# Kurtosis of 1,024 rows on one Trainium2 core: the queue by which the last results leave

## The chip, the core and the metric

The kernel runs on one core of a Trainium2 chip. Its time is device microseconds of that core for one execution, and a kernel's time is the median of several executions. The profile is of one execution. Its engines are TensorE (PE for matmuls, PEld for weight loads), VectorE (DVE), ScalarE (ACT), GpSimd (POOL) and SyncE (SP), which here only issues transfers and waits. A "q" behind an engine's name (SPq, ACTq) is the part of the engine that waits and issues, whose time isn't counted as busy.

## What is computed

The input is x, 1,024 rows of 8,192 float32 values, 33.5 MB. The output has one float32 for each row, 4 KB in all.

```
mean = np.mean(x, axis=-1, keepdims=True)
std = np.std(x, axis=-1, keepdims=True)
z = (x - mean) / (std + 1e-8)
return (np.mean(z ** 4, axis=-1) - 3).astype(np.float32)
```

So each row needs its mean, the sum of squares of the centred values, and the sum of their fourth powers. The whole input must be read once, and the output is four small stores.

## The kernel before, in words

The rows are cut into 18 groups (`GROUPS`). A group of k parts holds 128/k rows, each row cut into k pieces on k partitions, so that a group fills all 128 partitions with 8192/k columns. The first three groups have k = 8, 8 and 4 (less data, so that work starts early), the other fifteen k = 2, that is 64 rows and 4,096 columns each. A group is loaded into one of five buffers (`xt0` to `xt4`) by one to four transfers, all issued by SP (line 126). SP waits until a buffer is free, and that order is written out by hand in `load_next`.

For every group three things are done:

- The mean. In early groups DVE adds the two halves of the columns (line 149); in later ones PE transposes and sums 128-column blocks into PSUM (line 132) and DVE reduces pairs (line 138). A matmul with a small constant matrix gives minus the mean for each partition (lines 159 to 168), and ACT copies it to SBUF (line 170).
- The square. ACT computes (x - mean)^2 in place and keeps the sum (line 176).
- The fourth power. DVE squares and sums most of the columns (line 188), ACT the rest (line 183).

Results are put together for batches of groups (`BATCHES`): groups 0 and 1, group 2, groups 3 to 12, and groups 13 to 17. `factor` sums the squares of a row's pieces by matmul (lines 200 to 204) and takes minus the inverse square on DVE (lines 206 and 208). `scaled` multiplies the fourth-power sums by it (lines 215 and 216). `result` sums the pieces of a row by matmul with a selection matrix (line 226), subtracts 3 on DVE into the tile `kr` (line 228), and SP stores `kr` to `out` (line 230). For the last batch `kr` is 5 partitions of 64 values, 1.2 KB.

The batches before the last one are finished in steps between the groups. The last batch stands by itself at the end: ACT squares group 17 in two halves, DVE takes the fourth powers, ACT scales its share into `wa` (line 282), DVE its share into `w4` (line 284), and `result(b, [wa, w4])` accumulates both by two matmuls.

Line 313 of the profile is the end of the program, where the scope of the kernel is left. There SP waits for the eight semaphores on which transfers report, five wait instructions in all, and for DVE and ACT. In both builds the last of the five wait instructions holds the semaphore of the last store and the DVE count that comes with `kr`; the others hold semaphores of earlier transfers. Then all engines meet: each signals GpSimd, GpSimd releases them, the semaphores are cleared, and they meet again.

The statement that sets what the change touches is, in `result`:

```
nc.vector.tensor_scalar_add(kr, pk, -3.0)
dst = out[ROWS[b[0]]:ROWS[b[-1] + 1]].rearrange("(g r) -> g r", r=r)
nc.sync.dma_start(out=dst, in_=kr)
```

Of the kernel before, what the change touches and what calls it, by code (L numbers as in the profile page):

```python
# [43 lines left out]
def kernel(  # L44
# [5 lines left out]
    nc = tc.nc  # L50
# [4 lines left out]
    L = NG - 1  # L55
# [32 lines left out]
    for k in dict.fromkeys(k for k in KS if k > 2):  # L88
# [4 lines left out]
        out=ident, in_=ident, pattern=[[-1, P]], base=0,  # L93
# [125 lines left out]
    def result(b, terms):  # L219
        n = len(b)  # L220
        k = KS[b[0]]
        r = P // k
        sel = blk[k].rearrange("p (r k) -> p r k", k=k)[:, :, 0]
        pk = psfin.tile([n, r], f32, name="pk")
        for j, t in enumerate(terms):
            nc.tensor.matmul(pk, lhsT=t, rhs=sel, start=j == 0, stop=j == len(terms) - 1)  # L226
        kr = fin.tile([n, r], f32, name="kr")
        nc.vector.tensor_scalar_add(kr, pk, -3.0)  # L228
        dst = out[ROWS[b[0]]:ROWS[b[-1] + 1]].rearrange("(g r) -> g r", r=r)
        nc.sync.dma_start(out=dst, in_=kr)  # L230

    def finish(b):
        fac = factor(b)
        yield
        w4 = scaled(b, fac, len(b))
        yield
        result(b, [w4])
# [18 lines left out]
    for i in range(L):  # L256
# [12 lines left out]
    b = BATCHES[-1]  # L269
# [15 lines left out]
        out=w4[:, n - 1:], in0=qd[:, n:], scalar=qd[:, n - 1:n], in1=fac[:, n - 1:],  # L285
        op0=AO.add, op1=AO.mult)
    result(b, [wa, w4])


# [28 lines left out]
```

## Time and profile before

| what | value |
|---|---|
| median of 5 runs | 97.81 us (97.47 to 98.31) |
| the profiled execution's own time | 97.66 us |
| its span, first to last instruction | 95.9 us (95.943) |
| around the span | 1.72 us |
| ACT busy | 79.7 us, 83% |
| DVE busy | 76.2 us, 79% |
| PE busy | 57.4 us, 60% |
| HBM read | 33.55 MB, 350 GB/s over the span |
| last input packet | at 84.2 us |
| end of the last compute instruction (`kr`, line 228) | 93.9 us |

The views used are these. The page's slices cut the span in 40 equal parts with a digit for each engine's busy share. The chain of work that ended last follows the end of the program back through what released each step. The timeline lists instructions by start, with their length in us. The waits name who waited for whom: total us, times, longest. The list of a line gives the lengths of its instructions as minimum, median and maximum in ns. Starts and ends with three decimals are from the same trace's records, among them the landings: the moments at which a transfer's completion reaches its semaphore.

### The profile page before, as it was taken

The numbers are of one execution on the slowest core, as the hardware profiler recorded it, in microseconds if no ns is written. First come the engines' busy times: TensorE is split into PE (matmuls) and PEld (weight loads), VectorE is DVE, ScalarE is ACT, GpSimd is POOL, SyncE is SP. The second block draws the span as 40 slices with busy tenths as digits, with TensorE's granted clock in tenths as the row PEclk, the third lists the DMA queues.
The fourth block names the chain that finished last, engine by engine and source line by source line (L and its number), as shares of the span: only waits on it lengthen the run. The fifth ranks groups of instructions, "written<-read, shape, count | busy, mean of one in ns | idle before, by whom it ended". The sixth has DMA issues, their size and how long they took to land.

```text
span 95.9 us, 1268 instructions
## 1 busy us (share of the span) xinstructions
PE 57.4 (60%) x440; PEld 52.1 (54%) x440; DVE 76.2 (79%) x86; ACT 79.7 (83%) x89; POOL 4.6 (5%) x19
## 2 busy tenths in 40 slices
PE   0040202020299797979797979797978797961230
PEld 0040202020299696969696969696867686850210
DVE  2239449899992485989898989797989796999980
ACT  6055621999999499999999999999999898899960
POOL 6930000000000000000000000000000000000000
PEclk9999999999999999999999999999999999999655
DMA  2999999999999999999999999999999999400000
GB/s 68 377 398 454 437 430 437 430 424 395 407 409 393 439 421 431 423 422 412 432 412 435 417 409 421 401 419 410 418 413 418 407 418 406 171 3 0 0 0 4
DMA packets 5226, 33.63 MB, mean 351 GB/s; under 512 B 612, under 2 KB 612, under 8 KB 3812
## 3 DMA queue, kind: packets, MB, share of 16 engines
q1 hardware_dynamic: 5220, 33.56, 84.9%
q8 instruction: 3, 0.05, 0.2%
q14 instruction: 3, 0.02, 0.1%
HBM read 33.55 MB, written 0.00 MB: 350 GB/s over the span
## 4 chain that ended last, share of the span: by engine, by line
DMA 37%; ACT 25%; DVE 18%; PE 12%; issue 6%; SPq 0%; DVEq 0%
DMA xt<-in_x_dram 37%; ACT xt L176 21%; DVE xt L188 10%; PE tps L132 9%; DVE junk L149 6%; ACT xt L183 2%; PE mps L159 1%; PE mps L168 1%; DVE red L138 1%; ACT nmu L170 1%; PE pk L226 1%; ACT wa L282 0%; DVE qd L188 0%; DVE kr L228 0%; DVE fac L208 0%
## 5 line engine op out<-in xcount | busy, mean ns | idle before, releaser
L176 ACT ACTIVATE xt<-xt,nmu 128x4096 f32<-128x4096 f32 (+2 forms) x19 | 60.4, 3178 | 0.6
L188 DVE CUSTOM_DVE_ANT_0 xt<-xt 128x3456 f32<-128x3456 f32 (+7 forms) x19 | 58.9, 3102 | 1.7 <-ACT nmu L170 1.0
L132 PE MATMUL tps<-ident,xt 128*128 128x128 f32 x380 | 47.6, 284 | 0.5 <-DMA xt<-in_x_dram 0.3
L132 PEld LDWEIGHTS tps<-ident,xt 128*128 128x128 f32 x380 | 44.3, 148 | 2.1 <-DMA xt<-in_x_dram 1.8
L159 PE MATMUL mps<-part,blk 128*128 128x1 f32 x12 | 3.4, 350 | 23.1 <-DVE part L149 23.1
L159 PEld LDWEIGHTS mps<-part,blk 128*128 128x128 f32 x12 | 3.0, 311 | 23.4 <-ACT xt L176 9.2
L149 DVE CUSTOM_DVE_ANT_0 junk<-xt 128x2048 bf16<-128x2048 f32 (+3 forms) x7 | 10.0, 1427 | 6.3 <-DMA xt<-in_x_dram 6.3
L183 ACT ACTIVATE xt<-xt 128x640 f32<-128x640 f32 (+5 forms) x15 | 12.9, 858 | 0.5
L170 ACT COPY nmu<-mps 128x1 f32<-128x1 f32 x18 | 2.7, 150 | 11.2 <-PE mps L159 9.0
L138 DVE TENSOR_REDUCE red<-tps 128x128 f32<-128x256 f32 x12 | 5.1, 425 | 8.0 <-PE tps L132 7.9
L168 PEld LDWEIGHTS mps<-negcol,red 128*128 128x128 f32 x22 | 3.3, 188 | 8.9 <-ACT xt L176 5.7
L168 PE MATMUL mps<-negcol,red 128*128 128x1 f32 x22 | 3.9, 247 | 6.6 <-ACT xt L176 3.0
L176 ACT ACTIVATION_READ_ACCUMULATOR xt<-xt,nmu 128x1 f32 x19 | 3.5, 185 | 0.0
L183 ACT ACTIVATION_READ_ACCUMULATOR xt<-xt 128x1 f32 x15 | 2.8, 186 | 0.0
L70 ACT ACT_TABLE_LOAD x1 | 1.3, 1283 | 0.8 <-PEq L302 0.8
L83 POOL TENSOR_SCALAR_AFFINE_SELECT blk<-blk 128x128 f32<-128x128 f32 x3 | 1.7, 562 | 0.2
L80 POOL TENSOR_SCALAR_AFFINE_SELECT blk<-blk 128x128 f32<-128x128 f32 x3 | 1.7, 554 | 0.2
L201 PE MATMUL p<-s,blk 128*128 128x1 f32 x2 | 0.4, 260 | 2.1 <-ACT xt L176 2.1
L188 DVE DVE_READ_ACCUMULATOR2_ANT qd<- 128x1 f32 x19 | 1.6, 83 | 0.0
L202 PE MATMUL p<-s,blk 128*128 128x1 f32 x2 | 0.6, 363 | 1.6 <-ACT xt L176 1.6
L201 PEld LDWEIGHTS p<-s,blk 128*128 128x128 f32 x2 | 0.3, 188 | 2.2 <-ACT xt L176 2.2
L202 PEld LDWEIGHTS p<-s,blk 128*128 128x128 f32 x2 | 0.5, 313 | 1.7 <-ACT xt L176 1.7
(32 smaller groups left out, 13.0 us busy)
## 6 DMA issues: line engine op xcount, KB each, us to landing
xt<-in_x_dram SPq DMA_DIRECT2D x7, 1152.0 KB, 10.8
xt<-in_x_dram SPq DMA_DIRECT2D x9, 768.0 KB, 11.6
xt<-in_x_dram SPq DMA_DIRECT2D x7, 896.0 KB, 12.6
xt<-in_x_dram SPq DMA_DIRECT2D x3, 2048.0 KB, 11.0
xt<-in_x_dram SPq DMA_DIRECT2D x6, 512.0 KB, 11.3
xt<-in_x_dram SPq DMA_DIRECT2D x1, 1024.0 KB, 6.5
xt<-in_x_dram SPq DMA_DIRECT2D x1, 640.0 KB, 11.8
xt<-in_x_dram SPq DMA_DIRECT2D x1, 384.0 KB, 10.8
```

The costliest lines, as they stand in the source:

```text
L70: nc.scalar.activation(out=zeros[:, :1], in_=zeros[:, :1], func=AF.Square)
L80: nc.gpsimd.affine_select(out=v, in_=v, pattern=[[-k, r], [0, k]], base=0, channel_multiplier=1, compare_op=AO.is_ge, fill=0.0)
L83: nc.gpsimd.affine_select(out=v, in_=v, pattern=[[k, r], [0, k]], base=k - 1, channel_multiplier=-1, compare_op=AO.is_ge, fill=0.0)
L132: nc.tensor.matmul(tps, lhsT=xts[i][:, c:c + P], rhs=ident, start=c == 0, stop=c == w - P, is_transpose=True)
L138: nc.vector.tensor_reduce(out=red.rearrange("p (r k) -> p r k", k=2), in_=tps.rearrange("p (r k) -> p r k", k=2).unsqueeze(2).to_broadcast ...
L149: nc.vector.tensor_tensor_reduce(out=junk[:, :h], in0=t[:, :h], in1=t[:, h:], scale=1.0, scalar=0.0, op0=AO.add, op1=AO.add, accum_out=part)
L159: nc.tensor.matmul(mps, lhsT=blk[k], rhs=added_halves(i, 0), start=True, stop=True)
L168: nc.tensor.matmul(mps, lhsT=pair_sums(tps), rhs=negcol, start=True, stop=True)
L170: nc.scalar.copy(nmu, mps)
L176: nc.scalar.activation(out=t, in_=t, func=AF.Square, bias=nmus[i], accum_out=s2[:, j + extra:j + extra + 1])
L183: nc.scalar.activation(out=t, in_=t, func=AF.Square, accum_out=qa[:, j:j + 1])
L188: nc.vector.tensor_tensor_reduce(out=t, in0=t, in1=t, scale=1.0, scalar=0.0, op0=AO.mult, op1=AO.add, accum_out=qd[:, j + extra:j + extra ...
```

## The change

The store of the last batch is issued by ScalarE instead of SyncE. `b[-1] == L` holds for the batch that contains the last group alone; the three earlier stores stay with SyncE.

```diff
         dst = out[ROWS[b[0]]:ROWS[b[-1] + 1]].rearrange("(g r) -> g r", r=r)
-        nc.sync.dma_start(out=dst, in_=kr)
+        queue = nc.scalar if b[-1] == L else nc.sync
+        queue.dma_start(out=dst, in_=kr)
```

All lines behind it move down by one (282 becomes 283, 313 becomes 314). In the built program, the transfer becomes the last instruction of ACT before the end of the program, behind the scaling into `wa`; the semaphore that it reports on and the count that it waits for are as before. From SP's list the transfer goes, and with it a wait for that semaphore's earlier use. No other engine's order changes.

## The prediction

> **What bounds the kernel now.** I read the page's slices first, to see which stage the change is in; then the chain that ended last and the timeline of the last 4 us, for what stands on the path; then SP's waits, for who is late at the end; then the lengths of issues, for prices. The slices:
>
> ```profile
> DVE  2239449899992485989898989797989796999980
> ACT  6055621999999499999999999999999898899960
> DMA  2999999999999999999999999999999999400000
> GB/s 68 377 398 454 437 430 437 430 424 395 407 409 393 439 421 431 423 422 412 432 412 435 417 409 421 401 419 410 418 413 418 407 418 406 171 3 0 0 0 4
> ```
>
> The first 84 us are the loads with ACT and DVE beside them, the next 10 the arithmetic of the last groups, and in the last slice (2.4 us) ACT and DVE stand at 0, under a tenth. The change touches only that slice. The store that it moves is issued at 93.9 us, and by then the transfers have been idle for nearly ten us. So the loads, the buffers and the arithmetic keep their times, and what matters is the stretch from the last compute instruction to the end. The timeline of it (start us, length us, engine, line):
>
> ```profile
> 92.55 0.29 ACT L282 ACTIVATE wa<-qa,fac 128x1 f32<-128x1 f32 x1
> ...
> 93.29 0.38 PE L226 MATMUL pk<-blk,w 128*5 128x64 f32 x2
> 93.70 0.21 DVE L228 TENSOR_SCALAR kr<-pk 5x64 f32<-5x64 f32 x1 [0.47 <-PE pk L226]
> 93.94 0.29 SPq L230 DMA_DIRECT2D out_dram<-kr  x1
> ```
>
> `kr` ends at 93.910, its signal comes at 93.922, SP begins to issue at 93.938 (16 ns later) and is done at 94.231. ACT has nothing after 92.85. The packets, in a window from 93 to 97 us, whose 40 slices are 0.1 us each:
>
> ```profile
> DMA  0000000000000000000000002000000000000000
> GB/s 0 0 0 0 0 0 0 0 0 0 0 0 0 0 0 0 0 13 0 0 0 0 0 0 82 0 0 0 0 0 0 0 0 0 0 0 0 0 0 0
> ```
>
> The store's packets are the 13 in the slice from 94.7 (first packet 94.705, 0.474 us after the issue's end); the 82 at 95.5 is a fetch of instructions, which nobody waits for. The landings are at 95.047 to 95.103. What SP then waits for, from 75 us on (us in total, times, longest):
>
> ```profile
> SPq L230 <- DVE kr L228: 18.6, 2, 13.5
> SPq L313 <- PEq L313: 0.6, 2, 0.4
> SPq L313 <- DMA out_dram<-kr: 0.2, 1, 0.2
> ```
>
> The third row is the one to see: of its five waits at the end, SP stands only 0.2 us for the store itself. The four waits before it fill 94.277 to 94.886 and end 0.217 us ahead of the last landing (95.103 - 94.886). So the path is: `kr` signal 93.922; start 0.016; issue 0.293; to the first packet 0.474; to the last landing 0.398; SP passes its last wait at 95.119; from there to the span's end 95.943 is 0.824 us in which the engines meet.
>
> **The change part by part.** Each term is a difference to that path.
>
> 1. Start. ACT waits for the same DVE count. The nearest row is ACT's wait ahead of line 282: `fac`'s signal is at 92.242, ACT's wait record starts at 92.263, 21 ns later against SP's 16. Cost +0.005 us. Nothing is queued behind ACT's transfer but its signal at the meeting. This has cover: GpSimd needs all signals, SP's comes at 95.26, and ACT's issue would end near 94.24. Even with an issue of 1.06 us it ends at 95.0, and then the landing, which SP waits for, is later still. Without the cover, ACT's next instructions (17 and 14 ns) would cost under 0.1.
>
> 2. Issue. The page has no issue by ACT. The nearest rows are SP's own:
>
> ```profile
> L230 SPq DMA_DIRECT2D out_dram<-kr x4: 264/308/335, 52.3 to 93.9; - x4
> L126 SPq DMA_DIRECT2D xt<-in_x_dram x36: 327/328/1057, 0.8 to 74.5; - x36
> ```
>
> Lower bound: the shortest, 264 ns, is -0.029 against the 293 replaced. I see no reason why ACT should go under it. Upper bound: the longest, 1,057 ns, +0.764. A first use need not be slow: SP's first four loads took 402, 420, 419 and 432 ns, the first the shortest. I take the row nearest in shape, the store that is replaced: 0.
>
> 3. The queue. The page's DMA table has only q1 (SP's) and two queues of instructions; ACT's has not carried a packet. Nearest row: SP's first transfer, also on an unused queue, starts at 0.799, is issued in 402 ns and has its first packet at 1.844, 0.643 us after the issue's end. The last store needs 0.474. The difference, +0.169, is all that this trace has for an unused queue; it can be due to 128 partitions instead of 5, or to reading HBM instead of SBUF. Bounds: 0 and, if the issue's extra length counts too, +0.278 (1.045 - 0.767 from issue start to packet). I take +0.169, as the one row with an unused queue.
>
> The Trainium skill, "DMA: Bandwidth & Descriptors", section "Issuing engines are not separate DMA queues", says that transfers started by different engines run on the same 16 DMA engines and that a second issuer saves only issue time. Its section "Queues, rings and completion order" gives SP and ACT each a row of rings on those engines. By the first rule alone the store would cost what it does now, a change of 0, with nothing to save since SP has no other issue after 80.4; no run here shows it yet.
>
> 4. What SP loses: its issue, and a wait at 80.40 for the earlier use of the semaphore. SP can then run its four earlier waits as their transfers land, the last of them at 84.635, and stand at the fifth from then on. That takes 94.277 to 94.886 off SP, but this work is beside the store's flight already: gain 0, and at most nothing while the landing is later than 94.886. After the landing SP does the same five steps, 0.824 us.
>
> Other edits: none. ACT has one instruction more, SP two fewer.
>
> **Sum.** +0.005 + 0 + 0.169 + 0 = +0.17 us. Against the profiled execution: 97.66 + 0.17 = 97.83. That execution was 0.15 under the median; the change touches none of what may differ between executions, so I add the same sum to the median: 97.81 + 0.17 = 97.98. Half a per cent is 0.49 us, about what a measurement of this kernel can tell from no change. The forecast is inside it. Its own range comes from the bounds, -0.03 to +0.28, and 0.2 for a median's wander among runs spread from 97.47 to 98.31: 97.6 to 98.3.
>
> **The rivals.**
>
> - ACT's first issue is slow (slower than before). ACT has run only arithmetic for 94 us, and this would be the one transfer of its life in the program. For: no row shows an ACT issue, and SP once needed 1,057 ns where its neighbours took 328, so an issue is not bound to 0.3. Against: that long one fell beside a fetch of instructions (16 KB, from 41.518 on for 1.08 us), and SP's own first one was not long. Nothing covers it: every ns goes into the landing, and thence into the end. Price: 0.764 + 0.005 + 0.169 = +0.94, 98.75; with the queue's upper bound 1.05, 98.86. It decides from an issue of 0.293 + (0.49 - 0.17) = 0.61 us.
> - SP's work at the end is the bound (faster). If in other executions the landing comes before SP has done its four waits, or if the 1.72 us around the span hold work that hangs on SP's last transfer, then a free SP ends sooner. For: SP's four waits include one stall of 0.42 us (94.434 to 94.858), for which none of their semaphores is the cause, since these had been met by 84.64. Against: the third row of the waits has the landing last by 0.217 us. All that can be won in the span is the waits less that cover plus the issue's bound: even if the packets took no time, SP's waits took 0.61 us. Price: -0.6 at the very most in the span, 97.2; it decides only if the flight from issue to landing (1.165) gets shorter than 0.95, for which there's no row.
> - The change does nothing at all: ACT issues at SP's price on a queue at SP's price, so terms 1 to 3 are 0.005. This is 97.81. For: term 4 shows that the wait that ends last is the same, and the transfer has the same shape, semaphore and condition. Against: only the one row of term 3. That the store stays with SP after all is excluded: in the built program it is ACT's last instruction.
>
> **How the numbers follow.** The forecast (a little, up to 0.49 slower) 0.32; nothing at all 0.16; ACT's slow issue 0.38; SP's relief, with whatever isn't seen around the span, 0.14. I give the slow issue that much because it is the one term without any row of its own kind and without any cover. The time is the forecast's, 97.98. The range must reach to the slow issue (98.75, bound 98.86); of the faster case it takes in only a wander of the median, down to 97.4, which leaves out about 0.12 below and 0.07 above. Faster by over 0.5% 0.14; within 0.48; slower by over 0.5% 0.38.
>
> **What would show it.** In the profile after: an ACTq row for line 231 near 93.94, whose length says which case it is (0.26 to 0.34 the forecast, over 0.6 the rival); a new queue with 10 packets in the DMA table; the distance from the issue's end to the first packet (0.47 nothing, 0.64 the forecast); SP's four waits before 85, its fifth ending with the landing; 0.82 us from there to the end. I would be wrong if the landing isn't last, if ACT's signal is later than SP's, or if anything before 93.9 us has moved.

## The result and the profile after

The changed kernel takes 98.71 us (median of 36 runs, 97.70 to 99.82), the kernel before 97.93 us in the same comparison (71 runs). The ratio is 1.006, with a 95% interval of 1.0041 to 1.0079, that is 0.4 to 0.8 us slower. The ratio is of fast runs alone, without the ten runs of the changed kernel and the six of the kernel before that lie over 1.5% above that kernel's fastest, so it is smaller than the quotient of the medians, 1.008. The profiled execution took 98.50 us, its span is 96.784 us, and 1.72 us lie around it, as before.

First the slices of the changed kernel (the last one is again 0 for both engines), then the timeline of its last 4 us.

```profile
DVE  2245819899995094989898989897989997999960
ACT  6055260899999669999999999999999999999940
```

```profile
92.86 0.29 ACT L283 ACTIVATE wa<-qa,fac 128x1 f32<-128x1 f32 x1
...
93.58 0.38 PE L226 MATMUL pk<-blk,w 128*5 128x64 f32 x2
94.00 0.21 DVE L228 TENSOR_SCALAR kr<-pk 5x64 f32<-5x64 f32 x1 [0.47 <-PE pk L226]
94.24 0.56 ACTq L231 DMA_DIRECT2D out_dram<-kr  x1
```

The order of work is the same, and ACT now issues the store, in 0.56 us where SP took 0.29. `kr` ends at 94.208 instead of 93.910. That 0.298 can't be put down to the change: in three profiles of the changed kernel `kr` ends at 94.208, 93.601 and 94.785. So I measure everything from `kr`'s end on. From there to the end of the span it was 2.033 us, and it is 2.576, which is 0.543 more: nearly the whole of the 0.6%.

The store's packets, from the window 93 to 97 us of the changed kernel (0.1 us a slice), and their queue in the same window's table of queues:

```profile
GB/s 0 0 0 0 0 0 0 0 0 0 0 0 0 0 0 0 0 0 0 0 13 0 0 0 0 0 0 0 0 0 0 0 0 0 0 82 0 0 0 0
...
q10 hardware_dynamic: 10, 0.00, 0.2%
```

The 13 moved from 94.7 to 95.0, no more than `kr` did, though the issue is 0.26 us longer: the first packet leaves 0.795 us after the issue began (0.767 before), and 0.240 us after it ended (0.474 before). The last landing is at 95.441, 1.233 us after `kr`'s end instead of 1.193. Only 0.040 us of the loss lies up to here. The rest must be behind the landing.

Who SP waits for, from 75 us on, in the changed kernel:

```profile
SPq L314 <- DMA out_dram<-kr: 10.4, 1, 10.4
SPq L231 <- DVE kr L228: 5.5, 1, 5.5
SPq L314 <- DMA xt<-in_x_dram: 4.0, 3, 2.5
SPq L314 <- PEq L314: 0.6, 2, 0.4
```

SP's four earlier waits went ahead of the store as predicted (they start at 83.390 to 85.035), and SP then stands 10.4 us for the landing. The last row is the one to see. It was there before the change, with the same 0.6 and 0.4, and the name in it is wrong: PE's last instruction had ended at 94.006. The 0.4 is a stall of SP's that no semaphore explains. Where it stands is seen in the list of SP's instructions at the end (count, lengths as minimum, median, maximum in ns, first and last start). Before, from 94.4 to 94.95 us, the third and the fourth wait stand 0.45 us apart:

```profile
L313 SPq EVENT_SEMAPHORE  x2: 28/28/28, 94.4 to 94.9; - x2
```

Before, from 95.0 to 95.4 us, the fifth wait and the drains:

```profile
L313 SPq DRAIN  x2: 7/7/7, 95.2 to 95.3; - x2
L313 SPq EVENT_SEMAPHORE  x1: 28/28/28, 95.1 to 95.1; - x1
```

After, from 95.3 to 96.2 us:

```profile
L314 SPq DRAIN  x2: 7/64/121, 95.9 to 96.1; - x2
L314 SPq EVENT_SEMAPHORE  x1: 28/28/28, 95.5 to 95.5; - x1
```

In both the wait is SP's fifth, met by the last landing, and the second drain is SP's signal to the meeting of the engines. Before, the three start at 95.119, 95.189 and 95.253: 0.134 us from wait to signal. After, at 95.457, 95.912 and 96.094: 0.637. That is 0.503 us, and with the 0.040 it is the 0.543. Of the 0.503, 0.385 is the stall (0.455 instead of 0.070 from the wait to the first drain) and 0.118 goes with the first drain, which takes 121 ns instead of 7 (0.182 instead of 0.064 from it to the second). From the signal to the end of the span it is 0.690 us in both.

The stall came ahead of the fourth wait before the change (94.434 to 94.858) and comes ahead of the first drain after it (95.485 to 95.912). Counted in SP's records, both are the 80th: the change took two records from SP's list. In both, a fetch of 8 KB of instructions starts 0.64 us after the 80th record does (the 82 in the windows: 0.635 and 0.644).

So theory A: the stall belongs to a place in SP's list. Rival B: the store's way through ACT costs the half microsecond. Rival C: SP wakes slowly from a long wait.

### The profile page after: what moved, and what is told of

It is laid out like the page before. It is cut to its first block, busy times and chain, and to the rows that moved or that the text cites. A ratio compares the mean times of both kernels' runs of the same rounds, so it can differ in the third digit from the quotient of the medians.

```text
span 96.8 us, 1267 instructions
## 1 busy us (share of the span) xinstructions
PE 57.2 (59%) x440; PEld 52.4 (54%) x440; DVE 76.3 (79%) x86; ACT 79.6 (82%) x89; POOL 5.1 (5%) x19
## 4 chain that ended last, share of the span: by engine, by line
DMA 27%; ACT 24%; PE 20%; DVE 19%; issue 7%; SPq 0%; DVEq 0%; ACTq 0%
DMA xt<-in_x_dram 27%; ACT xt L176 21%; PE tps L132 16%; DVE xt L188 10%; DVE junk L149 5%; ACT xt L183 2%; DVE red L138 2%; PE mps L168 1%; PE mps L159 1%; PE pk L226 1%; ACT nmu L170 1%; SPq L126 0%; DVE w L216 0%; ACT wa L283 0%; DVE kr L228 0%
## 5 line engine op out<-in xcount | busy, mean ns | idle before, releaser
L132 PEld LDWEIGHTS tps<-ident,xt 128*128 128x128 f32 x380 | 44.8, 149 | 1.0 <-DMA xt<-in_x_dram 0.8
```

The source lines that it names most:

```text
L132: nc.tensor.matmul(tps, lhsT=xts[i][:, c:c + P], rhs=ident, start=c == 0, stop=c == w - P, is_transpose=True)
```

## The experiments

The value that each profile gives most sharply is the time from `kr`'s end to the span's end ("the tail").

| kernel | last store | stall stands | tail, us | ratio to before (95%) |
|---|---|---|---|---|
| before | SP | ahead of 4th wait | 2.033 | 1 |
| changed | ACT | behind 5th wait | 2.576 | 1.0060 (1.0041 to 1.0079) |
| changed, again | ACT | behind 5th wait | 2.576 | 1.0023 (0.9993 to 1.0053) |
| changed, third | ACT | behind 5th wait | 2.577 | 1.0067 (1.0028 to 1.0105) |
| pad1 | ACT | ahead of 5th wait (by the fetch) | 2.090 | 1.0008 (0.9973 to 1.0043) |
| pad2 | ACT | ahead of 4th wait | 2.082 | 1.0005 (0.9972 to 1.0039) |
| pad2, again | ACT | ahead of 4th wait | 2.077 | 1.0023 (0.9991 to 1.0054) |
| pad2, third | ACT | ahead of 4th wait | 2.071 | 1.0001 (0.9968 to 1.0033) |
| first_act | SP | behind 5th wait | 2.539 | 1.0064 (1.0036 to 1.0092) |
| first_act_pad2 | SP | ahead of 4th wait | 2.033 | 1.0017 (0.9988 to 1.0045) |
| first_pool | SP | behind 5th wait | 2.662 | 1.0048 (1.0018 to 1.0077) |
| first_pool_pad2 | SP | ahead of 4th wait (by the fetch) | 2.176 | 1.0039 (1.0005 to 1.0072) |
| all_act | ACT | none | 2.025 | 1.0024 (0.9982 to 1.0065) |
| act_split | ACT, in two | behind 5th wait | 3.093 | one run, 98.55 us |

### Two empty instructions, and one

The changed kernel, with empty instructions (drains) on SP behind the last line of the kernel (`pad2`; `pad1` has one). In the runs the first of them, right behind a transfer, takes 212 to 228 ns and a second one 7; SP only waits at that time, near 81 us.

```diff
     result(b, [wa, w4])
+    for _ in range(2):
+        nc.sync.drain()
```

> The changed kernel with two such empty instructions, as many as the change took from SP: the last store is ACT's, SP's list is as long as before. Theory A: the stall stands ahead of the fourth wait, as before the change, hidden near 85 us; 2.07 us from kr to the end, 1.000 to 1.002 of the kernel before, like the one with one. Rivals B and C: 2.58 us, 1.006.

> The changed kernel with one empty instruction (a drain, 7 ns elsewhere on SP) added to SP's list ahead of the end, so that the instruction behind SP's stall is its fifth wait and no longer the drain behind it. Theory A (the stall of 0.42 us belongs to a place in SP's instruction list, the 80th record, and the change moved it behind the last landing by taking two instructions away): the stall stands ahead of the fifth wait, near 85 us, SP's signal at the meeting comes 0.13 us after its wait, from kr's end to the span's end 2.07 us instead of 2.58, and the time is 0.5 us under the changed kernel's, 1.000 to 1.002 of the kernel before. Rival B (ACT's queue itself costs it, or whatever waits on a store of ACT's): 2.58 us and 1.006 stay. Rival C (SP wakes slowly after a long wait, here 10 us): the stall stays behind the fifth wait, 1.006 stays.

SP's end in `pad2`, first from 84.7 to 85.4 us (the third and fourth wait), then from 95.2 to 95.5 us (fifth wait and drains):

```profile
L316 SPq EVENT_SEMAPHORE  x2: 28/28/28, 84.8 to 85.3; - x2
```

```profile
L316 SPq DRAIN  x2: 7/7/7, 95.4 to 95.4; - x2
L316 SPq EVENT_SEMAPHORE  x1: 28/28/28, 95.3 to 95.3; - x1
```

The stall is now between the third and the fourth wait (84.806, 85.258), ten us ahead of the landing, and behind the fifth wait (95.297) the drains follow at 95.367 and 95.431. SP still stands 10 us for the store, and ACT still issues it, in 559 ns. So neither B nor C holds. The fetch has moved along; in the window 84 to 88 us of `pad2`, 0.1 us a slice, it is the 82 (85.897, 0.639 us after the 80th record):

```profile
GB/s 41 61 41 0 0 0 0 0 0 0 0 0 0 0 0 0 0 0 82 0 0 0 0 0 0 0 0 0 0 0 0 0 0 0 0 0 0 0 0 0
```

With one empty instruction the tail is 2.090. The 80th record is the fifth wait, which stands until the landing, so the stall itself can't be seen there. The fetch tells its place: it starts at 86.936, 1.093 us after the 79th record (1.087 in the kernel before), and so the stall ended more than nine us before the landing. Both kernels stand where the kernel before stands. 0.04 to 0.06 us remain in the tail, which is ACT's part.

### The mirror: SP's list shorter, the last store SP's

`first_act` is the kernel before with the store of the first batch on ACT, so that SP loses two instructions and nothing at the end changes engine:

```diff
-        nc.sync.dma_start(out=dst, in_=kr)
+        queue = nc.scalar if b[0] == 0 else nc.sync
+        queue.dma_start(out=dst, in_=kr)
```

> The mirror of the change: the first store (at 52 us) is ACT's and the last one is SP's. SP's list is two shorter, its waits at the end and their semaphores are as in the kernel before. Theory A: the stall of 0.42 us stands behind SP's fifth wait, though the store that it waits for is SP's own; 2.53 us from kr's end to the span's end, 1.005 of the kernel before. Rival B (the last store's way through ACT is what costs): 2.03 us, 1.000. ACT's early issue may add up to 0.5 us to either if ACT is the bound at 52 us; in the kernel with all stores on ACT three such issues and no stall came to 1.002.

> The same with two empty instructions (drains) given back to SP's list ahead of the last store. Theory A: the stall stands ahead of the fourth wait, within the store's flight; 2.03 us from kr's end to the span's end and 0.5 us less than the kernel without them, 1.000 to 1.002 of the kernel before. Rival B: no difference between the two.

SP's end in `first_act`, from 95.3 to 96.2 us, and in `first_act_pad2`, from 94.7 to 95.1 us:

```profile
L314 SPq DRAIN  x2: 7/64/120, 95.9 to 96.1; - x2
L314 SPq EVENT_SEMAPHORE  x1: 27/27/27, 95.5 to 95.5; - x1
```

```profile
L316 SPq DRAIN  x2: 7/7/7, 94.9 to 95.0; - x2
L316 SPq EVENT_SEMAPHORE  x1: 28/28/28, 94.8 to 94.8; - x1
```

The loss is there with SP's own store, as large as with ACT's (1.0064; tail 2.539), and SP waited only 0.6 us for that store. Given the two records back, the tail is 2.033 again. This is the cleanest pair: the half microsecond needs only the shorter list.

### The same with GpSimd

`first_pool` and `first_pool_pad2` are the same mirror with the first store on GpSimd (`nc.gpsimd if b[0] == 0`).

> The kernel before, last store by SP, with the first of the three early stores (at 52 us) issued by GpSimd, which takes two instructions from SP's list as the change does. Theory A: the stall of 0.42 us comes between SP's fifth wait and its drain though ACT issues nothing; from kr's end to the span's end 2.03 + 0.5 = 2.53 us; 1.005 of the kernel before. Rival B: 2.03 us and 1.000, since the store is SP's. Rival C: the same 1.000, since SP doesn't wait long at its end.

> The kernel with the first early store on GpSimd and the last on SP, with two empty instructions (drains) given back to SP's list ahead of the last store, so that the 80th record is the fourth wait again. Theory A: the stall stands ahead of SP's fourth wait, within the store's flight; from kr's end to the span's end 2.05 to 2.2 us instead of 2.66, and 1.000 to 1.001 of the kernel before instead of 1.005. Rival (the 0.5 us of that kernel was the price of GpSimd's store, not of SP's shorter list): 2.66 us and 1.005 stay.

The tail came and went as expected: 2.662 and 2.176. In `first_pool` the stall is seen behind the fifth wait. In `first_pool_pad2` the 80th record is itself held until the landing, and the stall's place follows from the fetch, 1.086 us after the 79th record. The times don't follow: 1.0048 and 1.0039, where 1.001 at most was expected of the second. GpSimd's store has a price of its own. In the tail it is 0.14 us against the kernel before (the landing's wait is the fourth here, and from SP's signal to the end it takes 0.738 us instead of 0.690); I haven't found the rest, the two intervals overlap, and the two kernels ran on different chips, each against the kernel before. As a test of times this pair decides nothing.

### ACT's issue

> The changed kernel with the last store cut in two that ACT issues one after the other (two rows of kr, then three): a look at what ACT's issue of 555 ns is. If it is a first use, the second issue takes 0.3 us, as SP's do; if it is ACT's price, both take 0.5 to 0.6. SP's list is as in the changed kernel, so the stall of 0.42 us stays behind the fifth wait under theory A.

`act_split` issues `kr[:2]` and `kr[2:]` one after the other on ACT. Its timeline of ACT from 93.7 to 95 us:

```profile
93.78 0.54 ACTq L232 DMA_DIRECT2D out_dram<-kr  x1
94.36 0.26 ACTq L233 DMA_DIRECT2D out_dram<-kr  x1
```

The long issue is a first use: 539 ns, then 256. The second store's issue begins 0.574 us after the first's and its last landing comes 0.531 us after the first's, which with the stall makes the tail 3.093.

> All four stores are issued by ACT; SP's list is then 78 records long, so the 80th is not reached before the end. Theory A: no stall in SP's list and no fetch of instructions in the last 10 us; from kr's end to the span's end 2.08 us, as in the changed kernel with one or two empty instructions. What ACT's three early issues cost in mid-run isn't known: 0.5 us each of ACT's order at least if ACT is the bound there, and its waits for kr, so 1.000 to 1.02 of the kernel before in all. First use: if ACT's 0.55 us is paid only once, the second to fourth issue take 0.25 to 0.35; if it is paid whenever arithmetic lies between, all take 0.55.

With all four stores on ACT (`nc.scalar.dma_start` in `result`), the lengths of ACT's issues are:

```profile
L230 ACTq DMA_DIRECT2D out_dram<-kr x4: 242/280/533, 51.5 to 94.9; - x4
```

The first takes 533 ns, the others 242, 292 and 267, though ACT computes for 10 to 20 us between them. The last store now lands 1.157 us after its issue began (SP's before: 1.165; ACT's first use: 1.201). SP's list has 78 records and no stall, and no fetch comes in the span's tail: the fetch is at 97.971, 1.08 us after the span's end. SP's fifth wait and its drains, from 95 to 96.3 us:

```profile
L313 SPq DRAIN  x2: 7/7/7, 96.1 to 96.2; - x2
L313 SPq EVENT_SEMAPHORE  x1: 28/28/28, 96.1 to 96.1; - x1
```

The tail is 2.025, the shortest of all, and still the time isn't below the kernel before (1.0024, 0.9982 to 1.0065). In the kernel before the stall is hidden too, so there is nothing to win.

### Whole times once more

> The changed kernel once more, beside the others of this call on one chip: 2.58 us from kr's end to the span's end, 1.004 to 1.008 of the kernel before under every theory; if it isn't, the chips differ and ratios of different calls can't be set side by side.

> The changed kernel with two empty instructions on SP once more, on the same chip as the changed kernel. Theory A: 2.08 us and 1.000 to 1.002, that is 0.5 us under the changed kernel. Rival: as the changed kernel.

> The changed kernel a third time. The end of it is 2.58 us from kr's end in every profile so far; the time up to kr's end varies by some tenths between executions, and in the last call it hid the difference to the kernel with two empty instructions (both 1.0023). Theory A: 1.003 to 1.008 of the kernel before, and 0.3 to 0.7 us above the other kernel of this call.

> The changed kernel with two empty instructions on SP a third time, beside the changed kernel. Theory A: 2.08 us from kr's end to the span's end, 0.999 to 1.003 of the kernel before, 0.3 to 0.7 us under the changed kernel. If the two are alike again, the end of the program isn't all that the times of whole executions show, and something ahead of kr gives the half microsecond back.

The first of these pairs missed: both 1.0023, with tails of 2.576 and 2.077. The second shows 1.0067 and 1.0001, medians of 98.59 and 98.07 us. The mean of the changed kernel's three ratios is 1.0050, that of the four of `pad1` and `pad2` 1.0009. The difference, 0.4%, is 0.40 us, near the 0.50 of the tails. What varies is the time up to `kr`, by over a microsecond between profiles (93.585 to 94.954), and one comparison of 12 runs can drown the effect in that.

## Why the prediction was right in its range and wrong in its cause

98.71 us lies in the range of 97.4 to 98.86, near its top; the forecast was 97.98. That it lies inside is luck: the range reached so far up for an issue by ACT that holds back the landing, and no issue did. The forecast's +0.17 had the right sign, but the 0.543 measured in the tail is three times as much, and 0.503 of it comes from a term that the sum had at 0.

- **The bound.** Right: only the stretch behind `kr` changed, the loads and the arithmetic keep their order.
- **Term 1, start, +0.005.** From `kr`'s end to the issue 0.028 before, 0.032 after. Right.
- **Term 2, issue, 0.** Wrong as a length: 555 ns against 293. But it isn't a term of the sum: the packets don't wait for the end of the issue's record.
- **Term 3, queue, +0.169.** Wrong. Measured from the start of the issue, the first packet is 0.028 later and the last landing 0.036. I had cut the flight at the end of the issue and priced both pieces apart, and what the first gained the second lost. The three terms together are 0.040, not 0.17. Once ACT has issued before, even this is gone (1.157 against 1.165).
- **Term 4, what SP loses, 0.** This is the step that failed: "After the landing SP does the same five steps, 0.824 us". They took 1.327, that is 0.503 more. I had seen the stall of 0.42 us, had noted that no semaphore explained it, and treated it as something that happens at that time. It is tied to a place in SP's list, and my own count ("SP two fewer") moved that place by two records, past the landing. Cover that had been there by luck, the store's flight, was gone.
- **The rival "ACT's first issue is slow".** It got the sign and most of the slower chance, by the wrong mechanism: the issue was longer, and nothing waited for it. By its own mark, 0.61 us, it wasn't reached either.
- **The rival "SP's work at the end".** It named the right object with the wrong sign: a freer SP didn't end sooner, since its stall moved behind the landing.
- **The rule of the Trainium skill** ("DMA: Bandwidth & Descriptors", "Issuing engines are not separate DMA queues") says that transfers run on the same 16 DMA engines whichever engine starts them. From it the prediction took that the store would cost the same from either engine. That fits the runs: from issue to landing 1.165 us from SP, 1.157 from ACT after first use, 1.201 at first use. The loss lay elsewhere.

Shown by the runs: the place of the stall in SP's list, and that moving it takes or gives the half microsecond, with either engine issuing the store. Only argued: that the stall is the crossing into another stretch of SP's program. For it speaks that, where the 80th record wasn't itself held by a wait, the 8 KB fetch follows it by 0.63 to 0.65 us (0.83 in `pad2`, again), and that no such fetch is in the span's tail where the list is shorter. The prediction called that fetch one "which nobody waits for"; it does start only after the stall is over, so SP doesn't stall for its data, but it goes with the stall. What SP does in those 0.43 us wasn't seen. The Trainium skill, "Runtime: NRT & Kernel Launch", section "Instruction fetch mechanics", has the engines refill instructions in 16 KiB blocks and calls the cost of crossing a boundary mostly hidden. The fetch that goes with SP's stall is 8 KB here. If the stall is such a crossing, its cost is hidden only where another wait covers it.

## What to carry to other kernels

When an edit adds or removes instructions on an engine, look for stalls in that engine's list that no semaphore explains, count at which record they stand, and ask what covers the same record after the edit; near the end of a program two instructions can be worth more than the edit itself. If such a stall falls on the path, an empty instruction or two puts it back under cover. And price a transfer from the start of its issue to its landing, in one piece.

## What the runs showed of the hardware that was not expected

- A stall of 0.43 us in SP's list ahead of its 80th record, in every profile in which the list is that long and no wait hides it. Where that record is the first drain at the end, this drain takes 120 to 125 ns (7 ns in the kernels with the stall elsewhere or none).
- ACT's first issue of a transfer takes 530 to 559 ns, its later ones 242 to 292 ns, and the long one delays the packets by only 0.03 us.
- The view of waits names a releaser for a stall that has none: "PEq 0.4" stands in the waits of both kernels, with PE long done.
